# Weights queued ahead of small constants, a masked spatial map made late, and the input rsqrt on VectorE, in a two-layer hybrid decoder step

## The chip, the cores and the metric

The kernel runs on all 8 cores of one Trainium2 chip, each core with its own sequence. The metric is the device time of the slowest core, in microseconds (us). Some executions of these kernels fall into a second, slower state: the cores of one die (sometimes of both) show a lower granted TensorE clock and the run is longer. Those executions are told apart by the span and clock of each core. Differences of under one per cent matter here, so I also use *milestones*: the time from the start of a core's span to a named instruction, as the median of the 8 cores of the profiled run.

## The reference

Two layers; each one is

```python
def mixer_block(h, ...):
    hn = rms_norm(h, norm_mix)              # x * rsqrt(mean(x^2) + 1e-6) * w
    proj = hn @ w_in                        # one wide input projection
    q, k, v, g_out, g_lr, xp, u, vv, gates = split(proj)
    # A: gated linear attention, a scan over chunks; per-head RMSNorm, output gate
    # B: trailing-window means of xp, starting from a 15-row history
    # C: spatial gate in chunks of 128: u * (tril(W_s) v + b)
    merged = ga*(A @ w_br_a) + gb*(B @ w_br_b) + gc*(C @ w_br_c)
    return h + merged @ w_out, ...
# then h = h + w_ff2 relu(w_ff1 rms_norm(h))^2
```

A core has 17 tiles of 128 tokens (16 of a prompt, one of 16 short sample sequences), in five blocks of 3, 3, 3, 4 and 4 tiles, and a width of 1024.

## The kernel before

A small scheduler issues the program in a fixed order for each engine. Background generators (`spawn`, `tick`) are interleaved with the foreground by counts of ticks, at build time. In the traces each engine runs its instructions in that order, and one that is not ready holds up those behind it on its engine (in the timeline of before, below, a copy of 0.19 us runs only after an operation that waited 8.79 us).

The order of the start. Inputs go out on SyncE's queue, weights on GpSimd's, and GpSimd queues the constants first:

```python
    for t in range(NXT):                 # NXT = 5 input tiles
        xdma(t)
        if t == 0:
            norm_w(0)
    rest_consts()                        # six small loads
    gla_consts(0)
    pump(6)                              # the first six weights
    x_e = spawn(load_x())
    while x_done[0] < 3:
        tick()
    norm_drain(0)
```

`gla_consts` makes four small loads into one buffer. The helper that issues a load waits for the previous writer of its buffer, so these loads wait for each other:

```python
    def gla_consts(l):
        plq.dma(wglr.t[:, :, 0:16], w_in_chunk(l, C_GLR, 16), writes=[wglr])
        for g in range(4):
            plq.dma(wgk2.t[32 * g:32 * g + 16, :], w_gk2[l], writes=[wgk2])
        spq.dma(nbg.t[:, :], b_gk[l], writes=[nbg])
```

The norm of a tile: sum of squares, logarithm and exponential on ScalarE, one multiplication on VectorE, eight transposes on TensorE, and an eviction on ScalarE:

```python
    def norm_stats(t, src, srcB, out, outB):
        ss = xss[:, t:t + 1]
        act(out, src, AF.Square, srcB, outB + [xssB[t]], acc=ss)
        act(ss, ss, AF.Ln, [xssB[t]], [xssB[t]], bias=EPS, scale=1.0 / D)
        act(ss, ss, AF.Exp, [xssB[t]], [xssB[t]], scale=-0.5)
        return ss

    def norm_tile(b, j, src, srcB, hb, lags, then=None):
        t = BLK[b][0] + j
        ss = norm_stats(t, src, srcB, hb.t[:, :], [hb])
        yield lags[0]
        stt(hb.t[:, :], src, ss, wn.t[:, :], ALU.mult, ALU.mult, srcB + [xssB[t], wn], [hb])
        ...
        yield lags[1]
        pe_transposes(...)               # hb -> PSUM
        act(hn_v(b)[...], pv..., AF.Copy, [ps], hnk[b])
```

The hand-over from the scan to the mixing: the spatial map and the pooling history are loaded when the sample scan ends, and the map is masked at once:

```python
    def mix_loads(l):
        spq.dma(wsp.t[:, :, :], w_spT[l].rearrange("g s t -> s g t"), writes=[wsp])
        for hf in range(2):
            spq.dma(hst.t[0:120, hf, :], spool[l, hf * 8:(hf + 1) * 8].rearrange("i r c -> (i r) c"), writes=[hst])
        spq.dma(pool_s[l][:, 0:7, :], spool[l][:, 8:15, :])

    def mix_prep(l):
        tt(wsT..., wsp..., cm..., ALU.mult, [wsp, cm], [wsT])      # masked map, VectorE
    # --- cut ---
        finish(smp_e)                    # the sample scan; it ends with mix_loads
        mix_prep(l)
        for b in range(NB):
            # --- cut ---
            mix_block(l, b)              # xp projections, u, history transposes, v, gates
```

## Time and profile before

| before | value |
|---|---|
| time | 2559.97 us median of 3 runs (2556.18 to 2946.33; the longest is a slow run) |
| span of the profiled run, slowest core | 2554.7 us |
| first projection starts (median of 8 cores) | 38.9 us |
| first k transposes of the scan | 109.8 us |
| sample scan ends | 313.0 us |
| first eviction of the mixing stage | 335.0 us |
| transposes of the pooling history | 350.0 us |

These lines are from the page of before: the span, then the busy time, share and instruction count of TensorE (PE), VectorE (DVE) and ScalarE (ACT).

```profile
span 2554.7 us, 40653 instructions; the slowest of 8 cores (2550.2 to 2554.7 us)
...
PE 2395.8 (94%) x13828; PEld 1257.5 (49%) x13828; DVE 1254.9 (49%) x2112; ACT 967.7 (38%) x1803; POOL 77.2 (3%) x98
```

TensorE is the bound. A change that leaves its matmuls alone can win little beyond the 6% in which it does not work (a little more where matmuls run slowly after a pause, see below).

The next lines are from the chain of waits of before, from the start to 56 us: start, length, what the chain went through.

```profile
5.14 12.31 DMA wgk_bf<-w_gk
...
17.99 3.93 DMA wgk_bf<-w_gk
...
22.44 1.92 DMA wgk_bf<-w_gk
...
25.35 12.82 DMA wring<-w_in
...
38.31 5.48 PE ps L219 x16
```

Three times a load waits for the load before it; only at 25.35 us does the first weight go out, and it takes 12.8 us. TensorE's first projection starts when it lands.

These are lines of the timeline of before: start, length, engine, line, operation, and in brackets the idle time before it and what ended that. The first group is from the start, the second from the input stage, the third from the hand-over, the last from the pooling.

```profile
9.45 1.04 ACT L190 ACTIVATE hbs_143<-xt_68 128x1024 bf16<-128x1024 f32 x1
...
20.34 0.83 PE L219 MATMUL ps<-hn,wglr 128*32 128x384 bf16 x8 [1.27 <-ACT hn L190]
...
38.31 5.46 PE L219 MATMUL ps<-wring,hn 128*128 128x512 bf16 x16 [17.14 <-DMA wring<-w_in]
...
94.37 0.21 ACT L190 ACTIVATION_READ_ACCUMULATOR hbs_142<-xt_67 128x1 f32 x1
94.66 1.28 ACT L190 ACT_TABLE_LOAD   x1
95.96 0.50 ACT L190 ACTIVATE xss<-xss 128x1 f32<-128x1 f32 x2
...
332.45 0.69 DVE L193 TENSOR_TENSOR wsT_p<-wsp,cm 128x512 bf16<-128x512 f32 x1 [8.79 <-DMA wsp<-w_spT]
...
333.32 0.19 DVE L202 COPY xf<-phist 128x60 f32<-128x60 f32 x1
...
333.60 0.39 ACT L190 ACTIVATE xf<-ps 128x256 f32<-128x256 f32 x1 [11.52 <-DVE xf L202]
...
334.31 2.72 PE L219 MATMUL ps<-hn,wring 128*128 128x384 bf16 x8 [10.96 <-ACT xfS L190]
...
343.14 0.17 DVE L193 TENSOR_TENSOR fix<-pt_115,invct 128x16 f32<-128x16 f32 x1
343.41 0.17 DVE L193 TENSOR_TENSOR pooled<-fix,xf 128x16 bf16<-128x16 f32 x1
```

Read them so. The third tile is normed at 20.3 us, where TensorE can do the small projection of the gates (its weights are there); then it waits 17.1 us for its first weight. In the input stage ScalarE loads another function table for one tile's `Ln` and `Exp`: the load takes 1.28 us, and from the end of the read before it (94.37 + 0.21 = 94.58) to the next activation it is 1.38 us. At the hand-over VectorE waits 8.8 us for the spatial weights; the small copy that ScalarE needs stands behind that in VectorE's order, ScalarE waits 11.5 us, and TensorE 11.0 us, until ScalarE's eviction `xfS` is done. After that pause its eight matmuls take 2.72 us (on each of the 8 cores). The table of windows gives TensorE a granted clock of 1.00 from 323.4 to 325.0 us in before, 0.50 from 327.0 to 338.5, and 1.00 again from 340.0. The last two lines show dependent small VectorE operations: 0.17 us each, 0.27 us from start to start.

The table of windows of before, for the stage between block 1's first projection and the scan: window, its length, and busy us (and count) of PE, PE's weight loads, DVE, ACT and GpSimd; then granted clock, DMA share and GB/s.

```profile
54.70:108.60 53.90, 47.88 (x309) 26.58 (x310) 29.79 (x54) 47.80 (x100) 0.00 (x0) 0.93 0.81 160
```

TensorE and ScalarE are both busy for nearly nine tenths of these 54 us, VectorE for a little over half.

And from the table of transfers of before, those issued in the first 8 us: size and the time from issue to landing.

```profile
xt_67<-xs SPq DMA_DIRECT2D x1, 512.0 KB, 4.9
...
xt_68<-xp SPq DMA_DIRECT2D x1, 512.0 KB, 6.6
xt_69<-xp SPq DMA_DIRECT2D x1, 512.0 KB, 7.7
```

### The profile page before, as it was taken

What the parts mean: (1) busy time and instruction counts of PE and PEld (TensorE: products, weight loads), DVE (VectorE), ACT (ScalarE), POOL (GpSimd) and SP (SyncE); (2) the same over time, 40 slices, a digit from 0 to 9 for tenths busy, and PEclk for the clock granted to TensorE, in tenths of its full rate; (3) what the DMA queues carried; (4) which work ended last, traced back from release to release, by engine and by line L of the source; (5) the groups of instructions that cost most, each with busy time, mean ns of one, the idle gap of its engine ahead of it and who ended that gap; (6) DMA issues with size and microseconds to landing.
All of it is one profiled execution on the core that took longest, in us unless ns stands there. A gap on an engine that the chain in (4) does not pass through costs nothing.

```text
span 2554.7 us, 40653 instructions; the slowest of 8 cores (2550.2 to 2554.7 us)
## 1 busy us (share of the span) xinstructions
PE 2395.8 (94%) x13828; PEld 1257.5 (49%) x13828; DVE 1254.9 (49%) x2112; ACT 967.7 (38%) x1803; POOL 77.2 (3%) x98
## 2 busy tenths in 40 slices
PE   3889979999999999999999898899999999999997
PEld 1544544555544545445555545455464454545453
DVE  2566655444445444444556666544443554444455
ACT  4866654322225311112555666532222441111133
POOL 1000000000000000000000000000000000000000
PEclk9999989999999999999999999999999999999999
DMA  9534732727236222315272347262450932222112
GB/s 178 107 100 125 138 80 75 149 63 128 83 64 168 42 34 34 43 24 68 76 146 84 96 119 133 75 133 79 77 116 32 214 59 33 34 34 33 17 50 91
DMA packets 176673, 219.27 MB, mean 86 GB/s; under 512 B 12978, under 2 KB 160826, under 8 KB 173368
## 3 DMA queue, kind: packets, MB, share of 16 engines
q0 software_dynamic: 81024, 78.07, 22.8%
q1 hardware_dynamic: 95448, 138.62, 17.2%
q8 instruction: 115, 1.88, 0.3%
q14 instruction: 86, 0.70, 0.1%
HBM read 240.12 MB, written 55.05 MB: 116 GB/s over the span
## 4 chain that ended last, share of the span: by engine, by line
PE 82%; DVE 5%; ACT 5%; DMA 4%; issue 3%; DVEq 0%; ACTq 0%; POOL 0%; SPq 0%; POOLq 0%
PE ps L219 81%; PE ps L228 1%; ACT L190 1%; DMA OB_d<-OBC_118 1%; DVE tmp_100 L196 1%; DMA wn<-nvec 1%; DMA wsp<-w_spT 1%; DMA wgk_bf<-w_gk 1%; ACT rsg L190 1%; DMA wring<-w_in 1%; DVE pt_115 L193 0%; DVE pt_116 L193 0%; DVE lv L661 0%; DVE go_85 L193 0%; ACT OBC_118 L190 0%
## 5 line engine op out<-in xcount | busy, mean ns | idle before, releaser
L219 PE MATMUL ps<-hn,wring 128*128 128x384 bf16 (+1 forms) x6400 | 1257.5, 350 | 37.1 <-ACT xfS L190 11.0
L219 PEld LDWEIGHTS ps<-hn,wring 128*128 128x128 bf16 x6400 | 623.1, 98 | 581.7 <-issue 56.4
L190 ACT ACTIVATE rl_139<-ps 128x384 f32<-128x384 f32 (+1 forms) x160 | 85.4, 534 | 487.5 <-PE ps L219 432.8
L219 PE MATMUL ps<-wring,a_1_138 128*128 128x512 bf16 x1088 | 238.6, 379 | 0.0
L219 PE MATMUL ps<-wring,a_0_137 128*128 128x512 bf16 x1088 | 238.3, 379 | 0.0
L219 PE MATMUL ps<-wring,hn 128*128 128x512 bf16 x848 | 205.1, 391 | 24.0 <-DMA wring<-w_in 17.1
L219 PEld LDWEIGHTS ps<-wring,a_0_137 128*128 128x128 bf16 x1088 | 106.3, 98 | 127.0
L219 PEld LDWEIGHTS ps<-wring,a_1_138 128*128 128x128 bf16 x1088 | 106.3, 98 | 126.3
L190 ACT ACTIVATE sg_133<-ps 128x384 f32<-128x384 f32 (+1 forms) x120 | 64.1, 534 | 237.3 <-PE ps L219 155.2
L190 ACT ACTIVATE sg_134<-ps 128x384 f32<-128x384 f32 (+1 forms) x120 | 64.1, 534 | 221.5 <-PE ps L219 156.5
L219 PEld LDWEIGHTS ps<-wring,hn 128*128 128x128 bf16 x848 | 81.8, 100 | 121.1 <-issue 40.7
L190 ACT ACTIVATE rl_140<-ps 128x384 f32<-128x384 f32 (+1 forms) x160 | 85.5, 534 | 138.8 <-PE ps L219 65.2
L193 DVE TENSOR_TENSOR tmp_135<-sg_133,ps 128x384 f32<-128x384 f32 (+1 forms) x80 | 48.6, 608 | 82.3 <-ACT sg_133 L190 44.4
L193 DVE TENSOR_TENSOR a_0_137<-rl_139 128x384 bf16<-128x384 f32 (+1 forms) x80 | 49.0, 612 | 80.8 <-ACT rl_139 L190 80.5
L193 DVE TENSOR_TENSOR a_1_138<-rl_139 128x384 bf16<-128x384 f32 (+1 forms) x80 | 48.9, 612 | 75.2 <-ACT rl_139 L190 74.6
L196 DVE SCALAR_TENSOR_TENSOR tmp_100<-ps,vec_t,rsg 128x512 f32<-128x512 f32 x68 | 51.0, 750 | 68.0 <-ACT rsg L190 60.6
L193 DVE TENSOR_TENSOR tmp_136<-sg_134,ps 128x384 f32<-128x384 f32 (+1 forms) x80 | 48.7, 609 | 68.8 <-ACT sg_134 L190 35.1
L193 DVE TENSOR_TENSOR a_1_138<-rl_140 128x384 bf16<-128x384 f32 (+1 forms) x80 | 48.9, 612 | 64.6 <-ACT rl_140 L190 63.9
L193 DVE TENSOR_TENSOR a_0_137<-rl_140 128x384 bf16<-128x384 f32 (+1 forms) x80 | 48.9, 612 | 63.9 <-ACT rl_140 L190 63.4
L219 PE MATMUL ps<-OBs_127,wring 128*128 128x384 bf16 (+1 forms) x320 | 72.5, 350 | 7.2 <-DVE acc_129 L193 7.2
L190 ACT ACT_TABLE_LOAD x55 | 70.6, 1283 | 21.7 <-PE ps L219 14.2
L190 ACT ACTIVATE hn<-ps 128x1024 bf16<-128x1024 bf16 x68 | 69.3, 1019 | 23.1 <-PE ps L228 22.9
(450 smaller groups left out, 2631.3 us busy)
## 6 DMA issues: line engine op xcount, KB each, us to landing
wring<-w_ff POOLq DMA_DIRECT2D x32, 1024.0 KB, 15.5
wring<-w_in POOLq DMA_DIRECT2D x30, 1024.0 KB, 15.5
H4s_125<-H_d SPq DMA_DIRECT2D x6, 768.0 KB, 15.0
OBs_127<-OB_d SPq DMA_DIRECT2D x6, 768.0 KB, 11.9
H4s_126<-H_d SPq DMA_DIRECT2D x6, 768.0 KB, 14.0
OBs_128<-OB_d SPq DMA_DIRECT2D x6, 768.0 KB, 5.6
Sf_90<-sgla SPq DMA_DIRECT2D x16, 256.0 KB, 3.0
Sf_91<-sgla SPq DMA_DIRECT2D x16, 256.0 KB, 2.9
```

Source lines behind the costliest of these rows:

```text
L190: return op(ACT, lambda: nc.scalar.activation(out=out, in_=in_, func=func, **kw), reads, writes)
L193: return op(DVE, lambda: nc.vector.tensor_tensor(out=out, in0=in0, in1=in1, op=alu), reads, writes)
L196: return op(DVE, lambda: nc.vector.scalar_tensor_tensor(out=out, in0=in0, scalar=scalar, in1=in1, op0=op0, op1=op1), reads, writes)
L219: inst = nc.tensor.matmul(m[0], m[1], m[2], start=m[3], stop=m[4], **kw)
L228: inst = nc.tensor.transpose(o, i, ident_ap)
```

## The change

Its intent: start TensorE earlier, by queueing the first weight (`v0`) ahead of all constants and unchaining the small loads; take the masked map off the hand-over; relieve ScalarE in the input stage, which is busy there and reloads tables, by computing the inverse square root of 11 input tiles on VectorE (an integer first guess and three Newton steps); and merge small matmuls. The diff, cut to its core:

```diff
+    def rsqrt(y, x, t, buf):
+        I32 = mybir.dt.int32
+        b = [buf]
+        v = nc.vector
+        ts(x, x, EPS, ALU.add, b, b)
+        op(DVE, lambda: v.tensor_scalar(out=t.bitcast(I32), in0=x.bitcast(I32), scalar1=1, scalar2=None, op0=ALU.arith_shift_right), b, b)
+        op(DVE, lambda: v.tensor_scalar(out=y.bitcast(I32), in0=t.bitcast(I32), scalar1=-1, scalar2=0x5F3759DF, op0=ALU.mult, op1=ALU.add), b, b)
+        for _ in range(3):
+            stt(t, y, -0.5, y, ALU.mult, ALU.mult, b, b)
+            tt(t, t, x, ALU.mult, b, b)
+            stt(y, t, 1.5, y, ALU.add, ALU.mult, b, b)
@@ memsets of constants now in set_consts(), called after block 0's norms @@
@@ gla_consts: each of the four loads writes a buffer of its own; nbg split off @@
-            plq.dma(wgk2.t[32 * g:32 * g + 16, :], w_gk2[l], writes=[wgk2])
+            plq.dma(wgk2.t[32 * g:32 * g + 16, :], w_gk2[l], writes=[wgk2g[g]])
@@ mix_loads: the history first, its halves unchained, then the map @@
-        spq.dma(wsp.t[:, :, :], w_spT[l].rearrange("g s t -> s g t"), writes=[wsp])
-        for hf in range(2):
-            spq.dma(hst.t[0:120, hf, :], ..., writes=[hst])
+        for hf in range(2):
+            spq.dma(hst.t[0:120, hf, :], ..., writes=[hstj[hf]])
+        spq.dma(wsp.t[:, :, :], w_spT[l].rearrange("g s t -> s g t"), writes=[wsp])
@@ norm_stats / norm_tile, for input tiles of blocks 2 to 4 (first=True) @@
+        if first:
+            act(out, src, AF.Square, srcB, outB + [xssB[t]], scale=D ** -0.5, acc=xst[:, 2 * t:2 * t + 1])
+            return ss
 ...
         yield lags[0]
+        if first:
+            rsqrt(ss, xst[:, 2 * t:2 * t + 1], xst[:, 2 * t + 1:2 * t + 2], xssB[t])
@@ load_x @@
-                norm_start(..., (1, 3) if b > 1 else (1, 1), ...)
+                norm_start(..., (1, 4) if b > 1 else (1, 1), ..., b > 1)
@@ o_norm: eight 128-wide sums become two 512-wide ones @@
-        for h in range(4):
-            for a in range(2):
-                pe_group([(ps.t[:, h * 128:(h + 1) * 128], ones_bf.t[:, :], sqg.t[:, 2 * h + a, :], a == 0, a == 1)], ...)
+        pe_group([(ps..., ones_bf.t[:, :], sv[:, a], a == 0, a == 1) for a in range(2)], ...)
@@ sgate: four bias matmuls become one 512-wide one, first in the group @@
@@ the start @@
+    pump(1)
+    gla_consts(0)
+    pump(6)
     for t in range(NXT):
         xdma(t)
         if t == 0:
+            nbg_load(0)
             norm_w(0)
-    rest_consts()
-    gla_consts(0)
-    pump(6)
@@ ... in layer 1 the first v0 projections come before the gates' low-rank one ... @@
@@ the map: made after the first v projection of block 0 instead of before the mixing @@
-        mix_prep(l)
+            if b == 0 and j == 0:
+                mix_prep(l)
```

More of the change, by code (lines that the diff above doesn't have):

```diff
@@ L312, in build_program @@
     wgk2 = sbc("wgk2_bf", [128, 512], BF16)
+    wgk2g = [B(wgk2.t) for _ in range(4)]
     wpm = sbc("wpm_bf", [128, 4, 128], BF16)
@@ L321, in build_program @@
     xss = nc.alloc_sbuf_tensor("xss", [128, NTILE], F32)
+    xst = nc.alloc_sbuf_tensor("xst", [128, 2 * NTILE], F32)
     xssB = [B(xss) for _ in range(NTILE)]
@@ L398, in build_program @@
     hst = sba("hst", [128, 2, 512], F32, RA)
+    hstj = [part(hst, hst.t, 2 * KB * j, 2 * KB) for j in range(2)]
     vtk = sba("vtk", [128, 4, 512], BF16, RA + 4 * KB)
@@ L427, in build_program, with set_consts @@
     memset(wglr.t[:, :, :], 0.0, [wglr])
-    memset(wgk2.t[:, :], 0.0, [wgk2])
-    for r_, n in ((resP, 4), (resS, 3)):
-        memset(r_.t[:, :], 1.0, [r_])
-        memset(r_.t[:, :].rearrange("p (j t) -> p j t", j=n)[:, :, 0:1], 0.0, [r_])
-    memset(resS.t[:, 0:128].rearrange("p (i t) -> p i t", t=LS)[:, :, 0:1], 0.0, [resS])
-    memset(bsp.t[:, :, :], 0.0, [bsp])
-    memset(bsS.t[:, :, :, :], 0.0, [bsS])
-    memset(ones_bf.t[:, :], 1.0, [ones_bf])
-    for h in range(4):
-        memset(eblP[h].t[:, 0:1], 1.0, [eblP[h]])
+    memset(wgk2.t[:, :], 0.0, wgk2g)
+    def set_consts():
+        for r_, n in ((resP, 4), (resS, 3)):
+            memset(r_.t[:, :], 1.0, [r_])
+            memset(r_.t[:, :].rearrange("p (j t) -> p j t", j=n)[:, :, 0:1], 0.0, [r_])
+        memset(resS.t[:, 0:128].rearrange("p (i t) -> p i t", t=LS)[:, :, 0:1], 0.0, [resS])
+        memset(bsp.t[:, :, :], 0.0, [bsp])
+        memset(bsS.t[:, :, :, :], 0.0, [bsS])
+        memset(ones_bf.t[:, :], 1.0, [ones_bf])
+        for h in range(4):
+            memset(eblP[h].t[:, 0:1], 1.0, [eblP[h]])
     def rest_consts():
@@ L449, in gla_consts, with nbg_load @@
         for g in range(4):
-            plq.dma(wgk2.t[32 * g:32 * g + 16, :], w_gk2[l], writes=[wgk2])
+            plq.dma(wgk2.t[32 * g:32 * g + 16, :], w_gk2[l], writes=[wgk2g[g]])
+    def nbg_load(l):
         spq.dma(nbg.t[:, :], b_gk[l], writes=[nbg])
@@ L460, in mix_loads @@
     def mix_loads(l):
+        for hf in range(2):
+            spq.dma(hst.t[0:120, hf, :], spool[l, hf * 8:(hf + 1) * 8].rearrange("i r c -> (i r) c"), writes=[hstj[hf]])
         spq.dma(wsp.t[:, :, :], w_spT[l].rearrange("g s t -> s g t"), writes=[wsp])
-        for hf in range(2):
-            spq.dma(hst.t[0:120, hf, :], spool[l, hf * 8:(hf + 1) * 8].rearrange("i r c -> (i r) c"), writes=[hst])
         spq.dma(pool_s[l][:, 0:7, :], spool[l][:, 8:15, :])
@@ L558, in norm_w, with norm_stats @@
         spq.dma(wn.t[:, :], nvec[k:k + 1, :].broadcast_to([128, D]), writes=[wn])
-    def norm_stats(t, src, srcB, out, outB):
+    def norm_stats(t, src, srcB, out, outB, first=False):
         ss = xss[:, t:t + 1]
+        if first:
+            act(out, src, AF.Square, srcB, outB + [xssB[t]], scale=D ** -0.5, acc=xst[:, 2 * t:2 * t + 1])
+            return ss
         act(out, src, AF.Square, srcB, outB + [xssB[t]], acc=ss)
@@ L565, in norm_stats, with norm_tile @@
         return ss
-    def norm_tile(b, j, src, srcB, hb, lags, then=None):
+    def norm_tile(b, j, src, srcB, hb, lags, then=None, first=False):
         t = BLK[b][0] + j
-        ss = norm_stats(t, src, srcB, hb.t[:, :], [hb])
+        ss = norm_stats(t, src, srcB, hb.t[:, :], [hb], first)
         yield lags[0]
+        if first:
+            rsqrt(ss, xst[:, 2 * t:2 * t + 1], xst[:, 2 * t + 1:2 * t + 2], xssB[t])
         stt(hb.t[:, :], src, ss, wn.t[:, :], ALU.mult, ALU.mult, srcB + [xssB[t], wn], [hb])
@@ L582, in build_program, with norm_start @@
     recent = []
-    def norm_start(b, j, src, srcB, bufs, lags, then=None):
+    def norm_start(b, j, src, srcB, bufs, lags, then=None, first=False):
         t = BLK[b][0] + j
@@ L587, in norm_start @@
             drain(recent[-len(bufs)])
-        e = spawn(norm_tile(b, j, src, srcB, bufs[t % len(bufs)], lags, then))
+        e = spawn(norm_tile(b, j, src, srcB, bufs[t % len(bufs)], lags, then, first))
         if j == 0:
@@ L612, in load_x @@
                 t = BLK[b][0] + j
-                norm_start(b, j, xt[t % NXT].t[:, :], [xt[t % NXT]], hb_start, (1, 3) if b > 1 else (1, 1),
-                           (lambda t=t: xdma(t + NXT)) if t + NXT < NTILE else None)
+                norm_start(b, j, xt[t % NXT].t[:, :], [xt[t % NXT]], hb_start, (1, 4) if b > 1 else (1, 1),
+                           (lambda t=t: xdma(t + NXT)) if t + NXT < NTILE else None, b > 1)
                 x_done[0] = t + 1
@@ L652, in gate @@
             ps = psum()
-            pe_group([(ps.t[:, 0:T], wgk2.t[:, h * 128:(h + 1) * 128], glr.t[:, 0:T], True, True)], [glr, wgk2], [ps])
+            pe_group([(ps.t[:, 0:T], wgk2.t[:, h * 128:(h + 1) * 128], glr.t[:, 0:T], True, True)], [glr] + wgk2g, [ps])
             g_, w = lv_.t[:, h, 0:T], [lvj_[h]]
@@ L664, in v0_gates @@
         def v0_gates():
-            vgrp(0, 0)
-            vgrp(0, 1)
+            if l == 0:
+                vgrp(0, 0)
+                vgrp(0, 1)
+                glrp()
+            else:
+                glrp()
+                vgrp(0, 0)
+                vgrp(0, 1)
             for h in range(4):
@@ L718, in kq @@
                 retire(l, "k", "q")
-        return glrp, v0_gates, v1, kq
+        return v0_gates, v1, kq
     def gla_gate(l, b):
@@ L743, in o_norm @@
         ps = psum()
-        for h in range(4):
-            for a in range(2):
-                pe_group([(ps.t[:, h * 128:(h + 1) * 128], ones_bf.t[:, :], sqg.t[:, 2 * h + a, :], a == 0, a == 1)], [sqg, ones_bf], [ps])
+        sv = sqg.t[:, :, :].rearrange("p (h a) t -> p a h t", a=2)
+        pe_group([(ps.t[:, :].rearrange("p (h t) -> p h t", h=4), ones_bf.t[:, :], sv[:, a], a == 0, a == 1) for a in range(2)], [sqg, ones_bf], [ps])
         act(rsg.t[:, :], ps.t[:, :], AF.Ln, [ps], [rsg], bias=EPS, scale=1.0 / 256)
@@ L949, in mix_block @@
                 pe_transposes([(ps.t[:, hf * 120:(hf + 1) * 120], hst.t[0:120, hf, g * 128:(g + 1) * 128]) for hf in range(2)],
-                              ident.t[0:120, 0:120], [hst, ident], [ps])
+                              ident.t[0:120, 0:120], hstj + [ident], [ps])
                 act(xfS.t[:, g, :, 0:15], ps.t[:, 0:240].rearrange("p (i r) -> p i r", r=15), AF.Copy, [ps], [xfS])
@@ L979, in sgate @@
         ps = psum()
-        mms = []
+        bv = bsS.t[:, :, :, :].rearrange("o g i t -> o (g i t)") if smp else bsp.t[:, :, :].rearrange("o g t -> o (g t)")
+        mms = [(ps.t[:, :], ones_bf.t[:, :], bv, True, False, True)]
         for g in range(4):
-            osl = ps.t[:, g * 128:(g + 1) * 128]
             wv = wsS.t[:, g, :] if smp else wsT.t[:, g, :]
-            bv = bsS.t[:, g, :, :].rearrange("o i t -> o (i t)") if smp else bsp.t[:, g, :]
-            mms += [(osl, vtk.t[:, j, g * 128:(g + 1) * 128], wv, True, False, True), (osl, ones_bf.t[:, :], bv, False, True, True)]
+            mms.append((ps.t[:, g * 128:(g + 1) * 128], vtk.t[:, j, g * 128:(g + 1) * 128], wv, False, True, True))
         pe_group(mms, [vtkj[j], ones_bf] + ([wsS, bsS] if smp else [wsT, bsp]), [ps])
@@ L1127, in build_program @@
     norm_drain(0)
+    set_consts()
+    rest_consts()
     for l in range(DEPTH):
-        mix_consts(l)
+        if l:
+            mix_consts(l)
         ts(nbg.t[:, :], nbg.t[:, :], -1.0, ALU.mult, [nbg], [nbg])
@@ L1153, in build_program @@
             p0[0]()
-            p0[1]()
             while x_done[0] < 6:
@@ L1158, in build_program @@
             p1[0]()
+            p0[1]()
             p1[1]()
             p0[2]()
-            p1[2]()
-            p0[3]()
             gla_gate(l, 0)
@@ L1167, in build_program @@
             pump()
+            mix_consts(l)
             gla_start()
@@ L1170, in build_program @@
             smp_e = spawn(gla_sample(l))
-            p1[3]()
+            p1[2]()
             gla_gate(l, 1)
@@ L1212, in build_program @@
                 gla_consts(l + 1)
+                nbg_load(l + 1)
             if s == 1 and b == 0:
```

## The prediction

> **What bounds the kernel.** The page shows TensorE busy 94% of the 2554.7 us span; 81% of the chain that ended last is its matmuls. The table of windows shows 95 to 100% TensorE from 400 us on, except in the second layer's scan (1400 to 1700 us, 88 to 92%). The change leaves gates and feed-forward alone, so it wins only idle time: the first 110 us and the hand-over to mixing near 320 us.
>
> **Removed.**
> 1. Start. The chain has w_gk2 loads waiting for each other (5.1 to 25.4 us) ahead of the first weights, which land at 38.2 us; the first projection starts at 38.3 us. Its three input tiles are normed at 20.2 us. With v0 queued first, sharing the DMA engines with the inputs (a weight took 12.8 us, an input tile 5 to 10), I expect it at 22 us: 16 us early.
> 2. Masked spatial map. In layer 1 VectorE waited 8.8 us for the spatial weights (18.2 us to landing), ScalarE 11.5 us for VectorE, TensorE 11.0 us (323.4 to 334.3), and the next eight matmuls ran cold, 2.7 us instead of 1.5. In layer 2 the load landed in 4.4 us and nobody waited. The history transposes came 15 us after the restart, so moved up they still find their loads. Gain 11 to 14 us, once.
> 3. ScalarE loses, for 11 tiles, Ln and Exp (0.50 us a pair) and four table loads at 94 to 103 us: about 10 us. [...]
>
> **Added.** rsqrt is 12 VectorE operations on 128x1, each waiting for the last. Small ones here (128x4, 128x16) take 0.16 to 0.17 us with 0.10 us before a dependent one: an estimate of 3.1 us a tile, 34 us for 11. They sit in order ahead of the evictions of v, k and q.
>
> **On the path.** From 55 to 108 us ScalarE was busy 47.6 of 53.4 us, VectorE 29.8. After: about 38 and 62, so VectorE becomes the limit. That stage should start 15 us earlier and last about 64 us instead of 53: the first scan transposes come at 100 to 107 us instead of 108.4. Most of the early start is given back; I count 4 us (-2 to +12).
>
> **Wide sums.** Eight 128-wide head-norm matmuls take about 0.46 us by issue, two 512-wide ones 0.43. The bias likewise. About 1 us in all. Deferred constants: about 0.
>
> **Sum.** 4 + 13 + 1 = 18 us from 2559.97: predicted 2541 us, range 2527 to 2553. Faster by over 2%: 0.04; within 2%: 0.95; slower: 0.01.
>
> **What would show it.** Timeline: first projection near 22 us; runs of 12 small VectorE operations, about 3 us per input tile; VectorE nearly gapless from 45 to 100 us, ScalarE with idle time; no table loads between the first gates; first k transposes at 100 to 107 us. Waits: none of VectorE for the spatial weights, no 11 us TensorE gap before the xp group. Layer 2 and the feed-forward within 2 us of before. Fewer matmuls, TensorE busy time almost unchanged.
>
> **What would make it wrong.** If dependent 128x1 operations take nearer 0.15 us, or VectorE's chains fit into its waits better than I think, the early start survives and the gain is near 30 us. If v0 and the input tiles slow each other so that norms end after 27 us, or the history loads hold up the transposes, it is under 12. If the first scan starts after 110 us, rsqrt costs more than the queue order wins.

In the page of before a table load takes 1283 ns. What item 2 calls "cold" is measured as 2.72 us at a granted clock of 0.50, against 1.46 us at 1.00. In the traces eight 128-wide matmuls take 0.45 us from their start to that of the next group (before, 342.25 to 342.70), two 512-wide ones 0.43 (after, 321.06 to 321.49).

## The result and the profile after

Ratios in this text are the mean time of one kernel's fast runs over the mean of the other's in the same rounds, so they are not quite the ratio of the medians. The medians of runs are over all of them, slow ones included.

| | before | after |
|---|---|---|
| median, us | 2558.51 (4 runs, 2556.18 to 2946.33) | 2550.48 (4 runs, 2548.31 to 2949.76) |
| ratio of fast runs | | 0.9969 (95%: 0.9946 to 0.9991) |

The change is 8 us faster (by the interval, 2 to 14), where 18 us were forecast. The milestones show where it went (median of 8 cores, profiled fast runs):

| milestone, us | before | after | difference |
|---|---|---|---|
| first projection | 38.9 | 26.8 | -12.1 |
| first k transposes of the scan | 109.8 | 113.7 | +3.9 |
| sample scan ends | 313.0 | 318.1 | +5.1 |
| first eviction of the mixing | 335.0 | 330.3 | -4.7 |
| history transposes | 350.0 | 343.6 | -6.4 |
| first branch gates | 469.6 | 463.3 | -6.3 |
| second layer's scan | 1343.0 | 1335.0 | -8.0 |
| end | 2552.0 | 2543.0 | -9.0 |

So 12 us are won at the start, 16 lost in the input stage, about 10 to 12 won at the hand-over, and 2 to 3 more come in small steps later on.

The page of after, the lines that answer to those of before:

```profile
span 2547.3 us, 40268 instructions; the slowest of 8 cores (2540.3 to 2547.3 us)
...
PE 2393.5 (94%) x13522; PEld 1243.2 (49%) x13522; DVE 1273.9 (50%) x2244; ACT 958.4 (38%) x1777; POOL 77.2 (3%) x98
```

TensorE has 306 matmuls fewer and 2.3 us less busy time; VectorE has 132 instructions more, the 12 times 11 of the inverse square root.

The chain of waits of after up to 120 us no longer shows the loads of `w_gk`. It waits for the second input tile, and from 53 us on it runs through VectorE, through the small operations (`xst`, `xss`) among others:

```profile
2.92 14.61 DMA xt_68<-xp
...
28.50 6.91 PE ps L232 x24
...
65.31 0.17 DVE xst L196
...
68.11 2.65 DVE lv L686 x3
...
83.35 0.33 DVE kq_78 L193
```

The timeline of after (its slowest core, which was among the later ones at the start): the start, a part of VectorE's row in the input stage, and the hand-over.

```profile
14.58 1.28 DVE L196 SCALAR_TENSOR_TENSOR hbs_142<-xt_67,xss,wn 128x1024 bf16<-128x1024 f32 x1 [10.44 <-DMA wn<-nvec]
...
17.61 1.06 ACT L190 ACTIVATE hbs_143<-xt_68 128x1024 bf16<-128x1024 f32 x1 [7.08 <-DMA xt_68<-xp]
...
28.50 4.85 PE L232 MATMUL ps<-wring,hn 128*128 128x512 bf16 x11 [1.27 <-ACT hn L190]
...
52.96 0.69 DVE L215 CAST v_81<-ps 128x512 bf16<-128x512 f32 x1 [1.36 <-PE ps L232]
53.57 0.14 DVE L199 TENSOR_SCALAR xst<-xst 128x1 f32<-128x1 f32 x1
53.83 0.15 DVE L207 TENSOR_SCALAR xst<-xst 128x1 int32<-128x1 int32 x1
54.09 0.15 DVE L208 TENSOR_SCALAR xss<-xst 128x1 int32<-128x1 int32 x1
54.36 0.16 DVE L196 SCALAR_TENSOR_TENSOR xst<-xss 128x1 f32<-128x1 f32 x1
...
56.47 0.16 DVE L196 SCALAR_TENSOR_TENSOR xss<-xst,xss 128x1 f32<-128x1 f32 x1
56.75 1.28 DVE L196 SCALAR_TENSOR_TENSOR hbs_142<-xt_68,xss,wn 128x1024 bf16<-128x1024 f32 x1
...
330.54 1.46 PE L232 MATMUL ps<-hn,wring 128*128 128x384 bf16 x8 [0.31 <-ACT go_85 L190]
...
333.22 0.39 ACT L190 ACTIVATE xf<-ps 128x256 f32<-128x256 f32 x1 [2.04 <-DVE xf L215]
...
333.92 1.46 PE L232 MATMUL ps<-hn,wring 128*128 128x384 bf16 x8 [1.48 <-ACT xfS L190]
```

Three readings. At the start TensorE's last wait is no longer for a weight but for the third normed tile; that is late because the norm weights and the second input tile landed late. From the square of the second tile to the first projection it is 28.50 - 17.61 = 10.9 us; in before, from the same square to the end of the third tile's norm, it was 20.3 - 9.45 = 10.9 us. So the work is the same, and it began 8 us later on these two cores, 5 us later by the medians of the 8 cores (15.9 against 10.7 us). In the input stage a tile's inverse square root is 12 operations, 0.26 us apart, 3.2 us from 53.57 to 56.75. At the hand-over the gap of 11 us has become 1.5 us and the eight matmuls take 1.46 us instead of 2.72.

The transfers of after (columns as before; the first line from the view of 0 to 3.2 us, the others of 0 to 20 us) show why the tiles are late:

```profile
wring<-w_in POOLq DMA_DIRECT2D x1, 1024.0 KB, 25.8
...
xt_67<-xs SPq DMA_DIRECT2D x1, 512.0 KB, 5.9
wn<-nvec SPq DMA_DIRECT2D x1, 512.0 KB, 12.0
xt_68<-xp SPq DMA_DIRECT2D x1, 512.0 KB, 14.6
xt_69<-xp SPq DMA_DIRECT2D x1, 512.0 KB, 17.4
```

On these two cores the second and third input tiles took 14.6 and 17.4 us where they had taken 6.6 and 7.7; by the medians of the 8 cores it is 12.9 and 15.1 against 8.0 and 9.5, some 1.6 times as long. The first weight, `v0`, was slowed even more: 24.5 us from issue to landing (median) against 13.1, so that it landed at 26.1 us, 0.5 to 1.7 us before the first projection of each core. The first input tile lost little (5.6 against 5.2). How the DMA engines divide their time between the queues no run shows; what the times show is that the second and third input tiles, issued by SyncE, land later beside the weight that GpSimd had queued a microsecond earlier, and the weight later beside them.

The window of the input stage of after, and below it the waits of its engines in nearly the same window (engine and its instruction, what it waited for, total us, times, longest):

```profile
47.20:116.35 69.15, 52.00 (x309) 27.96 (x309) 49.55 (x186) 38.73 (x73) 0.00 (x0) 0.90 0.65 126
```

```profile
DVE v_81 L215 <- PE ps L232: 9.1, 2, 7.7
ACT eb_73 L190 <- DVE xst L199: 7.0, 1, 7.0
```

The stage lasts 69.2 us instead of 53.9 (by the medians of the 8 cores, 68.8 instead of 54.8). ScalarE is indeed relieved, by 9.1 us, and VectorE has 19.8 us more. Its busy time does not show all of its load, since the 0.10 us between two dependent small operations counts as idle: over 11 tiles the chains hold VectorE for 11 x 3.2 = 35 us. Before the chains begin VectorE waits 9.1 us for block 1's first v1 projections, much as in before (9.7). ScalarE's first exponential of the cumulative gates now waits 7.0 us behind a chain.

One of the groups of these small operations, from the groups of VectorE in that window (shapes, count, then busy us and mean ns of one, then idle time before them):

```profile
L193 DVE TENSOR_TENSOR xst<-xst 128x1 f32<-128x1 f32 x33 | 5.2, 159 | 3.7 <-DVE xst L196 0.3
```

### The profile page after: what moved, and what is told of

Its sections match the earlier page's. It is cut to its first block, busy times and chain, and to the rows that moved or that the text cites. A ratio compares the mean times of both kernels' runs of the same rounds, so it can differ in the third digit from the quotient of the medians.

```text
span 2547.3 us, 40268 instructions; the slowest of 8 cores (2540.3 to 2547.3 us)
## 1 busy us (share of the span) xinstructions
PE 2393.5 (94%) x13522; PEld 1243.2 (49%) x13522; DVE 1273.9 (50%) x2244; ACT 958.4 (38%) x1777; POOL 77.2 (3%) x98
## 4 chain that ended last, share of the span: by engine, by line
PE 81%; DVE 7%; ACT 5%; issue 4%; DMA 2%; DVEq 0%; ACTq 0%; SPq 0%
PE ps L232 80%; PE ps L241 1%; ACT L190 1%; DVE tmp_100 L196 1%; DMA OB_d<-OBC_118 1%; DMA wn<-nvec 1%; ACT rsg L190 1%; DMA xt_68<-xp 1%; DVE pt_115 L193 0%; DVE lv L686 0%; DVE pt_116 L193 0%; ACT lv L190 0%; DVE U_96 L196 0%; DVE go_85 L193 0%; ACT OBC_118 L190 0%
## 5 line engine op out<-in xcount | busy, mean ns | idle before, releaser
L232 PE MATMUL ps<-hn,wring 128*128 128x384 bf16 (+1 forms) x6400 | 1256.4, 349 | 29.8 <-DVE kq_78 L193 9.1
L190 ACT ACT_TABLE_LOAD x51 | 65.4, 1283 | 22.4 <-PE ps L232 14.1
## 6 DMA issues: line engine op xcount, KB each, us to landing
wring<-w_ff POOLq DMA_DIRECT2D x32, 1024.0 KB, 14.7
H4s_125<-H_d SPq DMA_DIRECT2D x6, 768.0 KB, 15.1
```

The lines of the kernel that those rows point to most:

```text
L190: return op(ACT, lambda: nc.scalar.activation(out=out, in_=in_, func=func, **kw), reads, writes)
L232: inst = nc.tensor.matmul(m[0], m[1], m[2], start=m[3], stop=m[4], **kw)
```

## The experiments

My theory after the result: the start and the late map do what they should, and the inverse square root takes back more than the start gives, because VectorE takes its instructions in order and the evictions of v, k and q stand behind each tile's chain. The rivals: the early weights, not the arithmetic, slow the input stage through the DMA engines; the late map or the wide sums lose what is missing; or only VectorE's own busy time counts, so that the steps could be moved to an idle engine. Twelve kernels ran, on three chips. All outputs are right. "After", in what follows, is the changed kernel. The ratio is always to the kernel before on the same chip. A version with a power operation on VectorE instead of the Newton steps did not compile and never ran, so a cheaper exact form remains untried.

### e1: the change with the inverse square root back on ScalarE

```diff
-                norm_start(..., (1, 4) if b > 1 else (1, 1), ..., b > 1)
+                norm_start(..., (1, 3) if b > 1 else (1, 1), ...)
```

> The changed kernel with the input rsqrt put back on ScalarE (Ln, Exp, lags 1 and 3). Theory A (the 12-operation chains fill VectorE, which limits the input stage): the first scan transposes come at about 98 us (median of the cores) instead of 113.7, table loads between the gates return, total about 15 us below the changed kernel, ratio to before about 0.991. Rival B (weights and inputs sharing the DMA engines limit the stage): the first scan stays at 110 us or later and the total within 4 us of the changed kernel.

Measured: 2533.64 us against 2556.41, ratio 0.9903 (0.9875 to 0.9931), about 25 us faster than before. The first projection came at 26.0 us, 12.9 earlier than in before, and the first scan at 97.7, 12.1 earlier: nearly all of the early start survived the input stage. The window of that stage in this run, on its slowest core:

```profile
43.27:96.40 53.13, 48.02 (x308) 26.32 (x309) 29.78 (x54) 46.17 (x97) 0.00 (x0) 0.93 0.87 168
```

It is 53.1 us long against 53.9 in before (medians of the 8 cores: 53.2 against 54.8), with the same VectorE work as before and ScalarE again busy. So the queue order is not what slows the stage: with the early weights and without the chains it is as short as ever. The chains cost 113.7 - 97.7 = 16.0 us at the scan, and 2543.0 - 2528.3 = 14.7 us at the end.

### e3 and e4: one Newton step and six

```diff
-        for _ in range(3):
+        for _ in range(1):      # e3, less exact on purpose; e4: range(6)
```

> The changed kernel with one Newton step instead of three (6 operations a tile instead of 12, less exact on purpose). A: 6 x 0.264 x 11 = 17 us less VectorE time, first scan near 98 to 101 us because ScalarE then limits, total 12 to 16 us below the changed kernel. B: no change of the first scan.

> The changed kernel with six Newton steps (21 operations a tile). A: 9 x 0.264 x 11 = 26 us more VectorE time on the path, first scan at about 140 us, total about 26 us above the changed kernel (ratio to before about 1.007). B: under 5 us more.

Measured: with one step the first scan came at 96.6 us (a little before the expected 98 to 101), 17.1 earlier than after, and three of its four fast runs took 2533.4 to 2534.3 us (the fourth 2548.76, with two cores at a clock of 0.977 to 0.979; three more were slow; median of all 2548.76; ratio 0.9916, 0.988 to 0.9953). With six it came at 139.0, 25.3 later, and the ratio was 1.014 (1.0108 to 1.0172); some of this ratio is clock, for two cores of its profiled run had 0.972 instead of 0.982, and the other six ended at 2568.9 to 2574.6. The slopes are what counts. One step has 66 operations fewer: 17.1 / 66 = 0.26 us each. Six have 99 more: 25.3 / 99 = 0.26 us each. That is the distance from start to start in the trace. So in this range every small operation is on the critical path, at its full distance. Below it is not: e1 takes out the other 66 as well and gets no earlier (97.7). It also gives ScalarE its `Ln` and `Exp` back, so what limits the stage there was not separated.

### e10: the Newton steps on GpSimd

```diff
-            stt(t, y, -0.5, y, ALU.mult, ALU.mult, b, b)
-            tt(t, t, x, ALU.mult, b, b)
-            stt(y, t, 1.5, y, ALU.add, ALU.mult, b, b)
+            op(POOL, lambda: g.tensor_tensor(out=t, in0=y, in1=y, op=ALU.mult), b, b)
+            op(POOL, lambda: g.tensor_tensor(out=t, in0=t, in1=x, op=ALU.mult), b, b)
+            op(POOL, lambda: g.tensor_scalar(out=t, in0=t, scalar1=-0.5, scalar2=1.5, op0=ALU.mult, op1=ALU.add), b, b)
+            op(POOL, lambda: g.tensor_tensor(out=y, in0=t, in1=y, op=ALU.mult), b, b)
```

> The changed kernel with the Newton steps on GpSimd (4 operations a step), the three seed operations on VectorE. A (occupancy of VectorE): first scan at 97 to 104 us, like the ScalarE form. Rival C (the length of the chain from sum of squares to normed tile, wherever it runs): the chain is no shorter, so the first scan stays at 113 us or later.

Measured: 2568.82 us, ratio 1.0038 (1.0001 to 1.0075); first scan at 132.3, later than with the steps on VectorE (113.7). The timeline of this run shows the steps on GpSimd, and the view of waits, 45 to 125 us, what VectorE did meanwhile:

```profile
57.83 0.19 POOL L211 TENSOR_TENSOR xst<-xss 128x1 f32<-128x1 f32 x1 [2.71 <-DVE xss L208]
58.17 0.19 POOL L212 TENSOR_TENSOR xst<-xst 128x1 f32<-128x1 f32 x1
```

```profile
DVE hbs L196 <- POOL xss L214: 42.9, 10, 4.6
```

On GpSimd an operation on 128x1 takes 0.19 us, and 0.34 us from start to start. VectorE does only 3 of the operations, but waits 42.9 us for GpSimd, because the multiplication that needs the result is its next instruction. A chain is now about 5 us long instead of 3.2. So "VectorE has too much work" is too narrow a cause. What cost here was the length of the chain between two instructions that follow each other in VectorE's order, worked or waited. This says nothing about an order that leaves other VectorE work between the two; I had no run for that.

### e5, e6, e7: each part alone in the kernel before; e9: later weights held back

These four ran on a chip on which 16 of their 28 runs were slow (before: 2573.33 us, 2558.52 to 2946.49, granted clocks of 0.963 to 0.986 even in fast runs). Their total times are of little use, and I read their milestones of the first 350 us.

```diff
 # e5: before, with rsqrt() and first=True for blocks 2 to 4, lags (1, 4)
 # e6: before, with mix_loads reordered and unchained, mix_prep after the first v projection
 # e7: before, with the wide head-norm sums and the wide bias
 # e9: after, with:
     pump(1)
     gla_consts(0)
-    pump(6)
     for t in range(NXT):
         ...
+    POOL.wait(xt[2].w)          # third input tile has landed
+    pump(6)
```

> The kernel before with only the input rsqrt moved to VectorE (and its lag). Theory A: VectorE fills from 55 us on, the first scan comes at about 109.8 + 14 = 124 us, total about 14 us more than before, ratio 1.0055. Theory B: within 3 us of before.

Measured: first scan at 124.2 us instead of 109.8, 14.4 later; ratio 1.0149 (1.0117 to 1.0181), where 1.0055 was expected, with cores at clocks down to 0.961, so I don't use the total. The stage lasts 68.7 us (median of the 8 cores), as in after (68.8): the chains cost about as much in before's queue order as in the new one. This rules out that they are dear only because the early weights collide with them.

> The kernel before with only the late masked map and the unchained history loads ahead of it. The changed kernel gained 9.8 us between the last sample state and the first xp eviction, medians of the cores. If that gain is this part's alone: total 10 us less, ratio 0.996; my prediction had 11 to 14. If it came from an emptier DMA queue: under 5 us.

Measured: sample scan's end 313.1, first eviction of the mixing 325.1, history transposes 338.4: the gap to the first eviction fell from 22.0 to 12.0 us. The experiment moves the map and reorders the loads at once, but the load of the spatial weights was not made faster: in after it took 19.1 us to land, at 344.2 us (in before 18.2). A mask in its old place, before the evictions at 333 us, would still have waited for it, so the gain comes from the late place of the mask (357.6 us in after). The total was inconclusive on this chip (1.0005, 0.9949 to 1.0061), so I ran it again as e16.

> The kernel before with only the wide bias and head-norm sums. My count by issue is about 1 us in all; the changed kernel's second layer is 1 us shorter. Expected 0 to 2 us less, ratio 0.9992 to 1.0.

Measured: all milestones up to 350 us within about 1 us of before, ratio 1.0008 (0.998 to 1.0037). No effect can be told from zero.

> The changed kernel, except that GpSimd queues v1 and the weights after it only once the third input tile has landed. If sharing the DMA engines with the queued weights delays norm weights and input tiles: first projection at 21 to 24 us instead of 26.8 (median of the cores). Theory A then: the end of the stage is VectorE's, which starts 3 to 5 us earlier, so the total falls by 2 to 5 us. If it is v0 alone that delays them, no change.

Measured: first projection at 26.1 us, scan at 113.6; ratio 1.0029 (0.9969 to 1.0089). Nothing moved, so the five later weights do not delay the first normed tiles. What is left is v0 itself.

### e12 and e15: v0 held back too

```diff
-    pump(1)
     gla_consts(0)
-    pump(6)
     for t in range(NXT):
         ...
+    POOL.wait(xt[2].w)
+    pump(6)
```

> The ScalarE-rsqrt form of the changed kernel, with GpSimd queueing v0 and all later weights only once the third input tile has landed. If v0 itself, sharing the DMA engines, makes the norm weights and inputs late: norms of the first block end near 20 us again, v0 lands 12.8 us after about 10, and the first projection starts at 22 to 24 us instead of 26.0, total 2 to 3 us less than with v0 first. If what holds the first projection is something else: 26 us or later.

e12 is e1 with this; measured 2543.79 us against 2561.82, ratio 0.9934 (0.9919 to 0.9949). First projection at 30.8 us, scan at 101.4. From the timeline of this run:

```profile
19.64 1.01 PE L241 MATMUL ps<-ident_bf,hbs 128*128 128x128 bf16 x8 [4.33 <-DVE hbs L196]
31.57 4.66 PE L232 MATMUL ps<-wring,hn 128*128 128x512 bf16 x14 [10.93 <-DMA wring<-w_in]
```

Now the third tile is transposed at 19.6 us (18.1 in before), but TensorE then waits 10.9 us for the weight. So sharing is real: by the medians of the 8 cores the third tile is normed at 21.5 us here, as in before (21.4), and at 25.8 us in e1, 4.4 later. The weight, though, is a miss: on the slowest core it was queued at 13.5 us and took 17.9 to land, not 12.8, so the first projection came 7 us after the forecast of 22 to 24. Queueing v0 first is still the better of the two by 4 to 5 us, at the scan (97.7 against 101.4) as at the first projection (26.0 against 30.8). My forecast of 22 us took the best of both.

e15 is e14 (below) with the same edit:

> Both of these at once, as a candidate to beat both kernels: first projection as in the first, first scan 6 to 8 us before the 97.7 of the ScalarE form, ratio to before about 0.988.

Measured: 2540.81 us, ratio 0.9932 (0.9914 to 0.995), scan at 102.7. Against e14 on the same chip it is about 8 us slower. The scan shows 5 of these. One of its six runs (2550.53 us) had two cores at a clock of 0.972 to 0.973; without it the difference is 7 us. Where the rest comes from I did not find.

### e14: the chain for the last two tiles only

The last two tiles' `Ln` and `Exp` fall among the first output gates, where ScalarE reloads its table for each tile (1.28 us a load, two loads around one tile's pair in before: at 94.66 and 96.48 us). So I let only those two take the chain (everything else as e1):

```diff
-                           ..., b > 1)
+                           ..., t >= 15)
```

> The ScalarE-rsqrt form, with VectorE's chain only for the last two input tiles, whose Ln and Exp cost four table loads between the gates. Theory A says a chain costs only where VectorE limits, and there ScalarE does: first scan at 92 to 94 us instead of 97.7, total 4 to 5 us less, ratio to before about 0.9885. If a chain costs 3.1 us wherever it stands: no gain.

Measured: 2533.24 us, ratio 0.9898 (0.9881 to 0.9914), but the first scan came at 97.4 us, as in e1. This is a miss. From TensorE's row of the timeline of this run:

```profile
90.56 1.01 PE L241 MATMUL ps<-ident_bf,hbs 128*128 128x128 bf16 x8 [3.25 <-DVE xst L199]
```

The table loads between the gates are gone (none from 83.8 to 98.0 us on ScalarE), but TensorE waits 3.25 us for the last tile but one, whose transposes come soon after its chain in the order; what ScalarE gains, TensorE loses. At the end of the sample scan this run is 2 us earlier than e1 (301.4 against 303.7); the totals cannot be told apart (different chips).

### e16: the late map alone, again, on an undisturbed chip

The same kernel as e6.

> The kernel before with only the late masked map again, because the first chip it ran on was throttled (ratio 1.0005, 95% interval 0.9949 to 1.0061). Its trace there had the first xp eviction 9.9 us earlier and the first history transposes 11.6 us earlier. Expected total 10 to 12 us less, ratio 0.9955 to 0.996.

Measured: 2547.41 us against 2561.82, ratio 0.9954 (0.9939 to 0.9969), which is 11.8 us. First scan at 109.9 us, as in before; sample scan's end 313.0; first eviction 325.0; history transposes 338.3, 11.7 us earlier than before; first gates 458.8. The gain appears at one place and stays.

## Why the prediction was right or wrong

The forecast was a sum, and here is each term beside its measurement:

| term | predicted | measured | from |
|---|---|---|---|
| first projection earlier | 16 us | 12.1 us | milestones before and after |
| rsqrt, at the first scan | 11 us given back | 16.0 us given back | after against e1 |
| start and rsqrt together, at the first scan | 4 us gained (scan at 100 to 107) | 3.9 us lost (scan at 113.7) | milestones |
| late map | 13 us | 11.8 us | e16 |
| wide sums | 1 us | not to be told from 0 | e7 |
| total | 18 us | 8 us (9.0 at the end of the profiled runs) | ratio 0.9969 |

**Right.** The bound was right: 6.4 of the 9.0 us at the end of the profiled runs are there at 350 us, and little comes from the gates and the feed-forward. The start was rightly found in the chained small loads. The late map was right in place and mechanism, and nearly in size. The cost of one chain was right: estimated at 3.1 us a tile from two operations of the profile before, measured 3.2. The direction of the exchange was right as well, that VectorE becomes the limit of the stage and most of the early start is given back.

**Wrong.** The step that failed is "Most of the early start is given back; I count 4 us (-2 to +12)." Not most of it but all of it, and 4 us more. Two terms of that sum were mis-sized. (That the total still fell between 2527 and 2553 us is owed to the width of that range and to the late map, not to this step.)

First, "I expect it at 22 us: 16 us early" came out at 26.8 us. I took the norms as finished at 20.2 us from before and added little, though I named the sharing of the DMA engines in the same sentence. By the medians of the 8 cores the second tile landed at 15.9 us, and the 10.9 us of work from there on did not shrink. e9 and e12 show that it is v0 itself that delays the tiles: by 4 us (third tile normed at 25.8 us in e1, 21.5 in e12). The weight paid too: for it I had 12.8 us, and it took 24.5, so that it landed at 26.1 us. On its account alone 22 us would have been missed. The stage thus started 10.3 us earlier (median, 55.2 to 44.9 us), not 15.

Second, the stage was to "last about 64 us instead of 53". It lasted 69; by the medians of the 8 cores it grew by 14.0 us and not by 11, and this with the start accounts for the error at the scan. I added the chains (34 us) to VectorE's busy time (29.8 us), as if VectorE were then occupied from the first moment. But it first waits 9.1 us for block 1's projections, as it did before the change, and cannot use that time: the chains come after it in its order. Busy time plus wait plus chains, 29.8 + 9.1 + 35 = 74 us, is above the measured 69. In the trace the cast at 52.96 us lasts 0.69, and the next operation, which does not depend on it, starts at 53.57, an overlap of 0.08 us; if all 54 did so it would be 4 us: an estimate that fits, not a thing that a run shows. The dose of e3 and e4, 0.26 us per operation in both directions, shows that the chain lay on the critical path with its full length.

The prediction had listed this outcome: "If the first scan starts after 110 us, rsqrt costs more than the queue order wins." It did, on every core.

One of the two-input small operations takes 159 ns in the trace of after (the mean of 33). But that is busy time; what set the length of the dependent chain is 0.26 us from start to start.

**Where the gain of the queue order went.** Into VectorE's order: with `Ln` and `Exp` on ScalarE (e1), the same queue order and the same late map give about 25 us, three times what the change gives, and about the sum of the two terms (12.1 and 11.8), so that the deferred constants and the wide sums add little. e1 beats both kernels, and e14 does so by the same amount. The inverse square root on VectorE is a loss of about 15 us in this order of instructions, although it does take 9 us off ScalarE.

**Open.** Whether VectorE's chain would pay if other VectorE work were issued between the last Newton step and the multiplication, or if the steps of two tiles were computed in one set of operations; whether an exact form with fewer operations exists (the power form did not compile); what limits the stage once the chains are gone; and the last 2 to 3 us of e15 against e14.

## What to carry to other kernels

Here a chain of tiny dependent operations cost its length from start to start (0.26 us each), not its busy time (about 0.15), and it held up what was issued after it on its engine; moving the chain to an idle engine did not help (first scan at 132.3 us instead of 113.7), as the consumer stayed the next instruction. When work moves to an engine that looks half idle, look at *when* it is idle: add the chain to the waits that come before it, not only to the busy time. And when a load is moved to the front of the queues, estimate what it does to the landing of the transfers it overtakes: here the first weight won 12 us and not 16, because it and the inputs, both needed by the first projection, slowed each other (the weight took 24.5 us instead of 13.1, the second and third input tile 12.9 and 15.1 instead of 8.0 and 9.5).
